# Row sets by a table of places, blocks turned one by one at the peer head, operands shifted within 256 bytes

## The chip, the cores and the metric

The kernel is one program on one core of one Trainium2 chip. TensorE (PE) multiplies, VectorE (DVE) and ScalarE (ACT) work elementwise, GpSimd (POOL) issues the gathers, SyncE (SP) the other transfers; sixteen DMA engines move the data. The metric is the device time of one execution in microseconds. Before the change: median 2463.3 us of three runs (2456.23 to 2467.06).

## What is computed

One step of a streaming encoder in fp32 over 384 tokens: 256 of a prompt and 8 x 16 of running streams (the sample), 1024 wide. Layer 0 is a Mamba-2 mixer and a PEER channel mixer, layer 1 windowed attention and a PEER channel mixer; a norm ends it. The PEER part (128 x 128 experts, 8 heads, 16 picks each) is where most of the time goes:

```python
q = (xb @ w_q).reshape(PEER_TOKEN_BLOCK, PEER_HEADS, PEER_QDIM)
s1 = jnp.einsum('thd,nd->thn', q[..., :PEER_HALF], sub_k1)
s2 = jnp.einsum('thd,nd->thn', q[..., PEER_HALF:], sub_k2)
v1, i1 = lax.top_k(s1, PEER_TOPK)
v2, i2 = lax.top_k(s2, PEER_TOPK)
cand = (v1[..., :, None] + v2[..., None, :]).reshape(PEER_TOKEN_BLOCK, PEER_HEADS, PEER_TOPK * PEER_TOPK)
vs, ci = lax.top_k(cand, PEER_TOPK)
...
ue = jnp.take(u_tab, eid, axis=0)
act = jax.nn.gelu(jnp.einsum('tkd,td->tk', ue, xb).astype(jnp.float32))
ve = jnp.take(v_tab, eid, axis=0)
return jnp.einsum('tk,tkd->td', (gate * act).astype(xb.dtype), ve)
```

## The kernel before

**Stages.** Mixer, peer layer 0, attention, peer layer 1, final norm, one after the other. The tokens are three blocks of 128 (`NB`): two of the prompt, the third the sample.

**Products.** An fp32 product is made of three in the type fp32r: each operand is split in a rounded part `hi` and a rest `lo`, and hi·hi, hi·lo and lo·hi are summed in PSUM. `split` is two instructions, a copy on ACT (L130) and a subtraction on DVE (L131). Weights come in tiles of 512 KB, which SP issues (L150) into four `raw` buffers; `hi` and `lo` have two buffers each, and a third (`hix`, `lox`) where the dictionary `more` lends one. `gemm_cols` (L166 to L168) has the weights as the stationary operand and the activations as the moving one; `gemm_rows` (L179) the other way round.

**The mixer's and the attention's end.** The last product leaves the layer's result in six PSUM banks, two for each block. Behind it DVE adds them to the stream `h`: six instructions at L651 (mixer) or L914 (attention).

**A peer layer's head.** `rstd_of` (L192) gives 1/rms of each block: squares on ACT (L200), a sum on DVE (L202, L203), a power on POOL (L204). L951 norms a block, L968 transposes it on TensorE (24 transposes, eight banks), and `split` makes `qhi` and `qlo` of each bank. `exact` (L963, ACT) keeps an unsplit copy `xf`. Then sixteen column tiles of query products (`ct` 0 to 15, 384 columns) run, with the routing's top-16 on DVE beside and behind them.

**The U stage** is 128 steps, s = 0 to 127: in each a weight tile of the prompt's u table is loaded, split and multiplied with `qhi`/`qlo` (from s near 64 on with `xhi`/`xlo`). **The V stage** is another 128 steps, s = 128 to 255: the step's gated activations (`phi`, `plo`, from the array `G`) times a tile of the v table, into four PSUM banks of the prompt. Some tiles are *native*: unsplit fp32 (L1360).

**The sample's rows.** Each of the sample's 128 tokens has 128 picked experts, so rows are gathered by index instead: POOL issues indirect transfers (`gather`, L1168) of 128 rows of 4 KB, 0.5 MB each. 128 gathers bring u rows into three buffers `gath`, and DVE multiplies each (L1212, `u_item`). For v there are two ways. Of the 32 numbers r, 24 make *sets*: four gathers into free places of `G` (`fetch_v`), then eight matmuls of TensorE (`v_quad`, L1272) behind a small mask (`quad_prep`). The remaining eight r are 32 *items*: one gather each (`fetch_item`), and a multiply-add into `acc` on DVE (`v_item`, L1237); when the last is in, a mask is made (L1242, L1243) and TensorE reduces `acc` (L1247, `items_end`).

**What sets the order.** Tables at the head of the file say at which step s each thing is due: `U_DUE` (points of a line: so many u rows by such a step), `V_DUE` (the step of each set), `I_DUE` (first and last step of the items), `AHEAD` (up to which step the third weight buffer is lent). `tick`, `quads` and `item_tick` read them at each step. A place in the second half of `G` is free until the U step that fills it with gates, one in the first half from the V step on that has used them; `v_bufs` and the first line of `fetch_v` say which place the n-th row takes. The U stage's second half and the V stage run inside `in_order`, which fixes the order as written on PE, DVE and ACT (`HELD`); POOL and SP are not held. Elsewhere the framework's scheduler places the instructions; `behind` is one of its priorities.

Buffers lie in each partition in the order in which they are allocated, and with the sizes used here `xhi`, `xlo`, `qhi` and `qlo` all begin at a multiple of 256 bytes; so do their slices, 1024 or 1536 bytes apart.

## Time and profile before

| | us |
|---|---|
| median of three runs | 2463.3 (2456.23 to 2467.06) |
| the profiled execution | 2448.66 (its span 2447.0, mean granted TensorE clock 0.988) |
| mixer | 0 to 389 |
| head and query products of peer 0 | 389 to 502 |
| U stage, peer 0 | 502 to 895 |
| V stage, peer 0 | 895 to 1336 |
| attention | 1336 to 1492 |
| head and query products of peer 1 | 1492 to 1608 |
| U stage, peer 1 | 1608 to 1997 |
| V stage, peer 1 | 1997 to 2436 |
| final norm | 2436 to 2447 |

The table's stages are cut by hand, where the first matmul of the next kind stands. In the rows of the profile, times are microseconds from the span's start; a row names the engine, the line, the operation, the buffers (out<-in), the count, and in brackets the idle time ahead of it and what ended it. PEld is the loading of the stationary operand, which overlaps PE. The chain is the work that ended last, followed back from the end.

### The profile page before, as it was taken

The numbers are of one execution on the slowest core, as the hardware profiler recorded it, in microseconds if no ns is written. First come the engines' busy times: TensorE is split into PE (matmuls) and PEld (weight loads), VectorE is DVE, ScalarE is ACT, GpSimd is POOL, SyncE is SP. The second block draws the span as 40 slices with busy tenths as digits, with TensorE's granted clock in tenths as the row PEclk, the third lists the DMA queues.
The fourth block names the chain that finished last, engine by engine and source line by source line (L and its number), as shares of the span: only waits on it lengthen the run. The fifth ranks groups of instructions, "written<-read, shape, count | busy, mean of one in ns | idle before, by whom it ended". The sixth has DMA issues, their size and how long they took to land.

```text
span 2447.0 us, 44417 instructions
## 1 busy us (share of the span) xinstructions
PE 2356.0 (96%) x16592; PEld 2022.8 (83%) x16592; DVE 1967.0 (80%) x4237; ACT 1250.5 (51%) x2428; POOL 772.4 (32%) x779
## 2 busy tenths in 40 slices
PE   8999999999999999998998998999999999998997
PEld 7899988999998896666776777999998896666775
DVE  5988845979998999888775576979998998878775
ACT  5656524434476666454443554344476666554443
POOL 2222200012145434665442100011245435655540
PEclk9999999999999999999999999999999999999999
DMA  5555434466799889999994514456799889999994
GB/s 201 173 186 179 157 131 150 132 208 235 242 331 350 316 308 342 396 403 375 359 386 140 158 63 157 137 209 240 242 330 360 309 305 345 394 409 370 367 379 147
DMA packets 177080, 649.76 MB, mean 266 GB/s; under 512 B 21136, under 2 KB 23040, under 8 KB 174208
## 3 DMA queue, kind: packets, MB, share of 16 engines
q1 hardware_dynamic: 99936, 365.85, 41.7%
q0 software_dynamic: 76928, 281.07, 30.7%
q8 instruction: 130, 2.13, 0.3%
q14 instruction: 86, 0.70, 0.1%
HBM read 630.62 MB, written 18.06 MB: 265 GB/s over the span
## 4 chain that ended last, share of the span: by engine, by line
PE 65%; DMA 8%; DVE 5%; issue 3%; POOL 2%; ACT 2%; POOLq 0%; DVEq 0%; ACTq 0%
PE bank L179 20%; PE bank L166 11%; PE bank L168 11%; PE bank L167 11%; DMA gath<-in_p_u,eidU 4%; PE bank L1272 3%; PE bank L1360 2%; PE bank L1285 2%; PE bank L1327 2%; DVE lo L131 2%; DMA G<-in_p_v,eidU 1%; DMA G<-in_p_v,eidT 1%; POOL G L1168 1%; DMA G<-xrow 1%; DMA h<-hd 1%
## 5 line engine op out<-in xcount | busy, mean ns | idle before, releaser
L130 ACT CAST hi<-raw 128x1024 fp32r<-128x1024 f32 (+1 forms) x492 | 512.1, 1042 | 703.7 <-PE bank L167 373.8
L131 DVE TENSOR_TENSOR lo<-raw,hi 128x1024 fp32r<-128x1024 f32 (+1 forms) x492 | 595.4, 1211 | 170.0 <-ACT hi L130 165.3
L1168 POOL DMA_INDIRECT gath<-in_p_u,eidU x256 | 328.6, 1284 | 796.0 <-DVE gath L1212 448.4
L168 PE MATMUL bank<-xhi,lo 128*128 128x256 f32 (+1 forms) x1344 | 399.8, 297 | 8.6 <-DVE lo L131 8.6
L166 PE MATMUL bank<-xhi,hi 128*128 128x256 f32 (+1 forms) x1344 | 407.2, 303 | 0.0
L167 PE MATMUL bank<-xlo,hi 128*128 128x256 f32 (+1 forms) x1344 | 397.8, 296 | 0.0
L166 PE MATMUL bank<-qhi,hi 128*128 128x256 f32 (+1 forms) x896 | 272.9, 305 | 7.4 <-ACT xf L963 7.4
L168 PE MATMUL bank<-qhi,lo 128*128 128x256 f32 (+1 forms) x896 | 269.2, 301 | 1.0 <-DVE lo L131 0.9
L167 PE MATMUL bank<-qlo,hi 128*128 128x256 f32 (+1 forms) x896 | 269.6, 301 | 0.0
L1168 POOL DMA_INDIRECT G<-in_p_v,eidT x192 | 223.8, 1166 | 144.4 <-PE bank L1272 86.9
L168 PEld LDWEIGHTS bank<-xhi,lo 128*128 128x128 f32 x1344 | 256.6, 191 | 13.1 <-DVE lo L131 12.8
L166 PEld LDWEIGHTS bank<-xhi,hi 128*128 128x128 f32 x1344 | 256.9, 191 | 12.6 <-issue 7.1
L167 PEld LDWEIGHTS bank<-xlo,hi 128*128 128x128 f32 x1344 | 257.1, 191 | 0.3
L1212 DVE SCALAR_TENSOR_TENSOR gath<-gath,G 128x1024 f32<-128x1024 f32 x128 | 156.0, 1220 | 77.1 <-DMA gath<-in_p_u,eidU 76.8
L1315 ACT ACTIVATE oa<-ioh,e2T 128x128 f16<-128x128 f16 x512 | 163.3, 390 | 92.2 <-PE bank L1327 90.8
L179 PE MATMUL bank<-hi,phi 128*128 128x512 f32 x640 | 205.7, 403 | 0.2
L130 ACT CAST hix<-raw 128x1024 fp32r<-128x1024 f32 x104 | 109.1, 1049 | 188.4 <-PE bank L179 103.8
L179 PE MATMUL bank<-lo,phi 128*128 128x512 f32 x640 | 199.1, 392 | 3.6 <-DVE lo L131 3.6
L179 PE MATMUL bank<-hi,plo 128*128 128x512 f32 x640 | 197.7, 390 | 0.0
L166 PEld LDWEIGHTS bank<-qhi,hi 128*128 128x128 f32 x896 | 172.5, 193 | 8.1 <-ACT xf L963 7.9
L168 PEld LDWEIGHTS bank<-qhi,lo 128*128 128x128 f32 x896 | 172.4, 192 | 1.4 <-DVE lo L131 1.4
L131 DVE TENSOR_TENSOR lox<-raw,hix 128x1024 fp32r<-128x1024 f32 x104 | 126.9, 1221 | 57.4 <-ACT hix L130 57.3
(373 smaller groups left out, 4953.9 us busy)
## 6 DMA issues: line engine op xcount, KB each, us to landing
raw<-in_u_t SPq DMA_DIRECT2D x256, 512.0 KB, 4.6
raw<-in_p_v SPq DMA_DIRECT2D x256, 512.0 KB, 6.3
raw<-in_w_in SPq DMA_DIRECT2D x32, 512.0 KB, 4.2
raw<-in_p_w_q SPq DMA_DIRECT2D x32, 512.0 KB, 3.2
raw<-in_w_z SPq DMA_DIRECT2D x16, 512.0 KB, 5.2
s<-in_state_ssm SPq DMA_DIRECT2D x8, 1024.0 KB
out_sm_ssm<-s SPq DMA_DIRECT2D x8, 1024.0 KB, 5.2
raw<-in_w_out SPq DMA_DIRECT2D x16, 512.0 KB, 3.2
```

What stands on the lines that cost most here:

```text
L130: act.copy(hi, raw)
L131: dve.tensor_tensor(lo, raw, hi32, op=OP.subtract)
L166: pe.matmul(ps, whi[:, s], xhi[:, k, c0:c1], start=(k == 0), stop=False)
L167: pe.matmul(ps, whi[:, s], xlo[:, k, c0:c1], start=False, stop=False)
L168: pe.matmul(ps, wlo[:, s], xhi[:, k, c0:c1], start=False, stop=(k == KD - 1))
L179: mm = pe.matmul(ps, x, w[:, hf * n:(hf + 1) * n], start=s_, stop=e_)
L1168: pool.indirect_dma_start(out=tile_, out_offset=None, in_=tab, in_offset=bass.IndirectOffsetOnAxis(ap=idx, axis=0))
L1212: pin(dve.scalar_tensor_tensor(tile_, tile_, 1.0, xg[g], op0=OP.mult, op1=OP.mult, accum_out=au[g][:, j:j + 1]))
L1272: pe.matmul(out_s[hf][32 * q:32 * q + 32, :], cm[:, q], rows[q][:, hf * 512:hf * 512 + 512], start=(r == 0), stop=False, tile_position=(0, ...
L1285: pe.matmul(ps, wt[0][:, k * P:(k + 1) * P], xf[:, k], start=(k == 0), stop=(k == KD - 1))
L1315: act.activation(a[:, i], ioh, AF.Square, scale=-1.0, bias=e2T[:, t, 0:1])
L1327: pe.matmul(ps[:, i], ones[i // 4][:, i % 4], eg[:, i, j], start=(j == 0), stop=(j == 1))
```

## The change

Four parts, in the order of the diff.

1. *Tables and places.* The sets are due in three stretches: six in the U stage, seven from step 149 on, eleven from step 196 on (before 5, 11 and 8, from 83, 148 and 206 on). The places are now a table of their own, `V_SLOTS`: six in the second half of `G` from U step 36 on, eight in the first half from V step 133 on, each with the steps between which it may be used; `v_slot` gives a row the first one that is free, and `taken` holds those in use. One row is fetched at a step at most (before two). The line of u rows has more points, the items start six steps later and end four later, and the third weight buffer is lent three steps longer.
2. *The peer head.* The mixer and the attention hand their last add over (`hold["add"]`). The head does it block by block, inside `in_order`: add, squares, sum, power, norm, transposes, then the next block. The first weight tile is split ahead of it, with the third `hi`/`lo` buffer already lent. The query products of the first two column tiles (`ahead`) stand between the splits of the eight `k`. For the other tiles `behind` goes.
3. *The items' mask* is made when item 30 of 32 is in, in `items_sel`.
4. *Phases.* Small unused tiles are allocated ahead of or behind the operands. The mixer's `xhi`/`xlo` now begin 64 bytes past a multiple of 256, `qhi` 192, `qlo` 160, the peer's `xhi` 192 and `xlo` 224. The others stay at 0.

```diff
+I_DUE = (192, 250)
+AHEAD = 2 * 64 - 5
+U_DUE = ((64, 22), (71, 27), (78, 33), (104, 53), (128, 72), (148, 87), (196, P))
+V_DUE = ([82, 86, 90, 94, 98, 103] + [149 + 6 * i for i in range(7)] + [196 + 9 * (i // 2) for i in range(11)])
+V_SLOTS = [(1, 36 + 4 * i, 66, 100 + 4 * i) for i in range(6)] + [(0, e, 128 + e + 5, 256) for e in (0, 4, 8, 12, 20, 24, 28, 32)]
...
+            T(xp_pool, [P, 16], F32, tag="gap0")
             xhi = T(xp_pool, [P, KD, NT], F32R, tag="xhi")
             xlo = T(xp_pool, [P, KD, NT], F32R, tag="xlo")
+            T(xp_pool, [P, 48], F32, tag="gap1")
...
-                for b in range(NB):
+                def add(b):
                     for hf in range(2):
                         hh = h[:, b, hf * 512:(hf + 1) * 512]
                         dve.scalar_tensor_tensor(hh, accs[b][hf], rs[:, b:b + 1], hh, op0=OP.mult, op1=OP.add)
+
+                hold["add"] = add
...
+            gap = lambda n, i: T(qpool, [P, n // 4], F32, tag=f"gap{i}")
             sk = T(qpool, [P, 2, P], F32, tag="sk")
             sync.dma_start(sk, t_in["sub_k"][l])
+            gap(192, 0)
             qhi = T(qpool, [P, KD, NT], F32R, tag="qhi")
+            gap(224, 1)
             qlo = T(qpool, [P, KD, NT], F32R, tag="qlo")
+            gap(96, 2)
...
-            rr = rstd_of(h)
-            xn = []
-            for b in range(NB):
-                xn.append(qTp[:, 4 * b:4 * b + 4].rearrange("p c t -> p (c t)"))
-                after["dve"] = dve.tensor_scalar(xn[b], h[:, b], rr[:, b:b + 1], None, op0=OP.mult)
...
+            more.update(hi=(lpool, 1), lo=(lpool, 1))
+            turn_of.update(hi=1, lo=1)
+            raws = [load_raw(t_in["p_w_q"][l, ct]) for ct in range(2)]
...
+            def squares(b):
+                for hf in range(2):
+                    hh = slice(hf * 512, hf * 512 + 512)
+                    act.activation(xn[b][:, hh], h[:, b, hh], AF.Square, scale=1.0 / 32, accum_out=s2[:, b, hf:hf + 1])
+
+            def normed(b, parts):
+                c = slice(b, b + 1)
+                dve.scalar_tensor_tensor(ss[:, c], s2[:, b, 0:1], EPS, s2[:, b, 1:2], op0=OP.add, op1=OP.add)
+                pool.tensor_tensor(rr[:, c], ss[:, c], mhalf[:, c], op=OP.pow)
+                for i in range(parts):
+                    w = slice(i * D // parts, (i + 1) * D // parts)
+                    dve.tensor_scalar(xn[b][:, w], h[:, b, w], rr[:, c], None, op0=OP.mult)
...
+            with in_order():
+                wq = [split_raw(raws[0])]
+                for b in range(NB):
+                    add(b)
+                    squares(b)
+                    normed(b, 1 + (b == 2))
+                    if b < 2:
+                        turn(range(2 + 2 * b), [0] if b == 0 else [1])
+                    if b == 1:
+                        turn((2, 3), [0])
...
-            for k in range(KD):
-                ps = bank([P, NT])
-                for b in range(NB):
-                    pe.transpose(ps[:, b * P:(b + 1) * P], xn[b][:, k * P:(k + 1) * P], ident)
-                turned.append(ps)
-                split(qhi[:, k], qlo[:, k], ps, scale=gcol[:, 2 + l, k:k + 1])
-                if k == 1:
-                    exact(0)
...
+            with in_order():
+                turn((4, 5), [0, 1])
+                turn(range(6), [2])
+                ahead = [bank([P, NT]) for _ in range(2)]
...
+                act.copy(hi1, raws[1])
+                for k in range(KD):
+                    ready(k)
+                    if k in (1, 2):
+                        exact(k - 1)
+                    ks = slice(k * P, (k + 1) * P)
+                    pe.matmul(ahead[0], wq[0][0][:, ks], qhi[:, k], start=(k == 0), stop=False)
+                    pe.matmul(ahead[1], hi1[:, ks], qhi[:, k], start=(k == 0), stop=False)
+                    pe.matmul(ahead[0], wq[0][0][:, ks], qlo[:, k], start=False, stop=False)
+                    pe.matmul(ahead[1], hi1[:, ks], qlo[:, k], start=False, stop=False)
+                    pe.matmul(ahead[0], wq[0][1][:, ks], qhi[:, k], start=False, stop=(k == KD - 1))
+                    if k in (1, 2):
+                        turn([k + 5], range(NB))
+                for k in range(2, KD):
+                    exact(k)
+                dve.tensor_tensor(lo1, raws[1], hi1.bitcast(F32), op=OP.subtract)
+                for k in range(KD):
+                    pe.matmul(ahead[1], lo1[:, k * P:(k + 1) * P], qhi[:, k], start=False, stop=(k == KD - 1))
...
-                half, e = (1, HE - 20 + 4 * (n % 4)) if s < 2 * HE else (0, 4 * (n % v_bufs(s)) + (4 if n % v_bufs(s) > 3 else 0))
...
+            def v_slot(n, s):
+                return next((k for *k, s0, s1 in V_SLOTS if s0 <= s and V_DUE[n // 4] <= s1 and tuple(k) not in taken), None)
...
-            def items_end():
+            def items_sel():
...
+                    if done["i"] == TG - 2:
+                        items_sel()
...
-                last = 4 * V_FIRST if s < 2 * HE else 4 * len(QR)
-                ahead = 4 * done["v"] + (4 if s < 2 * HE else v_bufs(s))
-                for _ in range(2):
-                    n = done["f"]
-                    if n < min(ahead, last) and (n < 4 * V_FIRST or s > 2 * HE + 4 + 4 * (n % 4)):
-                        fetch_v(n, s)
-                        done["f"] += 1
+                first = 4 * sum(d < 2 * HE for d in V_DUE)
+                if s % 4 == 3 and s < V_DUE[0]:
+                    return
+                if done["f"] < (first if s < 2 * HE else 4 * len(QR)) and v_slot(done["f"], s):
+                    fetch_v(done["f"], s)
+                    done["f"] += 1
...
                     xhi = T(xp, [P, KD, NP], F32R, tag="xhi")
+                    T(xp, [P, 8], F32, tag="gap")
                     xlo = T(xp, [P, KD, NP], F32R, tag="xlo")
...
-                if e2 >= 7:
+                if e2 >= 2:
                     quads(HE + e2)
```

What moves on three engines follows; lines of the changed file from 653 on lie 2 to 76 further down.

DVE at the first peer head, before: `h` is the stream, `ss` a block's mean square, `qTp` the normed block. Adds of the later blocks (L651) stand ahead of the first block's norm (L951).

```order
L651 SCALAR_TENSOR_TENSOR h_95<-bank_3484,rs_3953,h_95 128x512
L202 TENSOR_TENSOR ss_3989<-ss_630_3990 128x1
L203 TENSOR_SCALAR ss_3989<-ss_3989 128x1
L651 SCALAR_TENSOR_TENSOR h_95<-bank_3485,rs_3953,h_95 128x512
L651 SCALAR_TENSOR_TENSOR h_95<-bank_3486,rs_3953,h_95 128x512
L951 TENSOR_SCALAR qTp_3987<-h_95,rstd_3991 128x1024
```

The same place after (L653 is the add, L976 the sum, L980 the norm):

```order
L131 TENSOR_TENSOR lox_3999<-raw_3991,hix_3998 128x1024
L653 SCALAR_TENSOR_TENSOR h_95<-bank_3485,rs_3955,h_95 128x512
L653 SCALAR_TENSOR_TENSOR h_95<-bank_3486,rs_3955,h_95 128x512
L976 SCALAR_TENSOR_TENSOR ss_3995<-ss_637_3996 128x1
L980 TENSOR_SCALAR qTp_3986<-h_95,rstd_3997 128x1024
L653 SCALAR_TENSOR_TENSOR h_95<-bank_3487,rs_3955,h_95 128x512
```

A block is normed ahead of the next block's add, and the first weight split stands ahead of all of it.

POOL in the V stage of layer 0, where sets and u rows are gathered, before: `G<-in_p_v,eidT` is a row of a set, `gath<-in_p_u` a u row.

```order
L1168 DMA G_624_3979<-in_p_v,eidT_3975 128x1024 x4
L1168 DMA gath_11979<-in_p_u,eidU_3968 128x1024
L1168 DMA G_624_3979<-in_p_v,eidT_3975 128x1024
L1168 DMA gath_12015<-in_p_u,eidU_3968 128x1024
L1168 DMA gath_12063<-in_p_u,eidU_3968 128x1024
L1168 DMA G_624_3979<-in_p_v,eidT_3975 128x1024 x4
L1168 DMA gath_12099<-in_p_u,eidU_3968 128x1024
```

After, the queue there:

```order
L1233 DMA G_626_3975<-in_p_v,eidT_3971 128x1024 x4
L1233 DMA gath_11929<-in_p_u,eidU_3964 128x1024
L1233 DMA G_626_3975<-in_p_v,eidT_3971 128x1024
L1233 DMA gath_11968<-in_p_u,eidU_3964 128x1024
L1233 DMA gath_12005<-in_p_u,eidU_3964 128x1024
L1233 DMA gath_12046<-in_p_u,eidU_3964 128x1024
L1233 DMA gath_12125<-in_p_u,eidU_3964 128x1024
L1233 DMA G_626_3975<-in_p_v,eidT_3971 128x1024 x5
```

There are four u rows between two groups of set rows where there were one or two; the set rows still stand four and five in a row.

DVE at the last items of layer 1, before: L1237 is an item, `cm` the mask, L131 the splits of the weights and of the gates.

```order
L131 TENSOR_TENSOR lo_27180<-raw_27177,hi_27179 128x1024
L131 TENSOR_TENSOR plo_27184<-G_3436_20031,phi_27183 128x256
L1237 SCALAR_TENSOR_TENSOR G_2848_16531<-G_2848_16531,cU_16522 128x1024
L1242 MEMSET cm_27200 128x128
L1243 TENSOR_REDUCE cm_27200<-ident_69 128x4x8
L131 TENSOR_TENSOR lo_27226<-raw_27223,hi_27225 128x1024
```

After (L1303 the item, L1308 and L1309 the mask):

```order
L1303 SCALAR_TENSOR_TENSOR G_2847_16522<-G_2847_16522,cU_16513 128x1024
L1308 MEMSET cm_27212 128x128
L1309 TENSOR_REDUCE cm_27212<-ident_69 128x4x8
L131 TENSOR_TENSOR lox_27218<-raw_27215,hix_27217 128x1024
L131 TENSOR_TENSOR plo_27222<-G_3432_20023,phi_27221 128x256
L131 TENSOR_TENSOR lo_27240<-raw_27237,hi_27239 128x1024
L131 TENSOR_TENSOR plo_27244<-G_3432_20023,phi_27243 128x256
L1303 SCALAR_TENSOR_TENSOR G_2847_16522<-G_2847_16522,cU_16513 128x1024 x2
L131 TENSOR_TENSOR lo_27284<-raw_27281,hi_27283 128x1024
```

The mask has moved ahead of two weight splits, and the last two items stand together.

## The prediction

> **What bounds the kernel now.** The page comes first: the engines' shares, the chain that ended last, the sizes of the transfers.

> ```profile
> PE 2356.0 (96%) x16592; PEld 2022.8 (83%) x16592; DVE 1967.0 (80%) x4237; ACT 1250.5 (51%) x2428; POOL 772.4 (32%) x779
> ...
> PE 65%; DMA 8%; DVE 5%; issue 3%; POOL 2%; ACT 2%; POOLq 0%; DVEq 0%; ACTq 0%
> ...
> raw<-in_p_v SPq DMA_DIRECT2D x256, 512.0 KB, 6.3
> ```

> TensorE works or is waited for nearly always, so only two things shorten the kernel: its remaining waits, and a shorter matmul. DMA is second in the chain. So I looked next where TensorE stands still and DMA ends the wait: the V stage (the 128 V steps of a peer layer). These are its steps 24 to 71 of layer 0 (s = 152 to 199 in the code), and two later stretches, for the product matmuls alone; the columns are the stretch, its length, busy time (count) of PE and PEld, the granted clock, the DMA share, GB/s.

> ```profile
> 975.20:1162.00 186.80, 122.47 (x492) 92.28 (x493) 0.98 0.99 392
> 1209.40:1260.50 51.10, 44.10 (x194) 35.88 (x193) 1.00 0.95 369
> 1260.50:1282.20 21.70, 21.70 (x97) 17.98 (x96) 1.00 1.01 397
> ```

> The last row is eight undisturbed steps: 96 matmuls in 21.70 us, 0.226 us each. The middle one is sixteen steps (192 matmuls, 43.4 us) with four sets of v rows: (51.1 - 43.4) / 4 = 1.92 us a set. The other work of the first stretch follows, by line: native V tiles (L1360), the row sets (L1272, 16 records each), the gate products (L1327), POOL's gathers (L1168).

> ```profile
> 975.20:1162.00 186.80, 25.63 (x56) 10.23 (x56) 0.98 0.99 392
> 975.20:1162.00 186.80, 22.64 (x160) 4.74 (x160) 0.98 0.99 392
> 975.20:1162.00 186.80, 12.37 (x309) 10.34 (x305) 0.98 0.99 392
> 975.20:1162.00 186.80, 110.50 (x90) 0.98 0.99 392
> ```

> TensorE needs 492 x 0.226 + 25.6 + 12.4 + 10 x 1.92 = 168.4 us there, but the stretch lasts 186.8: 18.4 us are lost. DMA needs (90 gathers + 48 weight tiles) x 0.524 MB = 72.4 MB, at 392 GB/s 184.6 us. **The stretch runs at DMA's pace**, at a share of 0.99. How the loss looks at its worst point, on PE and then on DVE:

> ```profile
> 1139.01 0.61 PE L179 MATMUL bank<-hix,phi 128*128 128x512 f32 x2
> 1145.53 1.22 PE L179 MATMUL bank<-lox,phi 128*128 128x512 f32 x2 [5.90 <-DVE lox L131]
> 1146.55 1.05 PE L179 MATMUL bank<-hix,plo 128*128 128x512 f32 x2
> 1147.40 1.05 PE L179 MATMUL bank<-hix,phi 128*128 128x512 f32 x2
> ...
> 1143.10 1.23 DVE L1212 SCALAR_TENSOR_TENSOR gath<-gath,G 128x1024 f32<-128x1024 f32 x1 [6.27 <-DMA gath<-in_p_u,eidU]
> ```

> VectorE, whose order is fixed, stands 6.27 us at an item for its late row; the split of the next weight tile stands behind it, and TensorE behind that. After it, pairs of matmuls begin 0.85 us apart (1146.55, 1147.40) instead of 2 x 0.226 = 0.45.

> **The change part by part.** *Row sets.* Stepping through both versions' tables gives, for s = 152 to 199, 89 gathers before (the trace shows 90) and 78 now: 38 u rows, 33 v rows, 7 item rows; 8 sets instead of 10. TensorE's need falls to 168.4 - 3.8 = 164.6 us, DMA's to (78 + 48) x 0.524 = 66.1 MB, 168.5 us at 392 GB/s. DMA still ends last, by 4 us: gain 186.8 - 168.5 = 18.3. What was removed comes back at s = 200 to 239: 8 sets instead of 6, 54 gathers instead of 45. TensorE needed 480 x 0.226 + 6 x 1.92 = 120.0 and needs 123.8 us now; DMA (54 + 40) x 0.524 = 49.3 MB, 125.7 us. Cost 5.7. Net 12.6 us a layer; the same stretch of layer 1 also has 492 such matmuls in 186.8 us: **-25 us** for both. The ends come from the rate. At 397 GB/s (the 1260.50 row) the two stretches take 166.4 and 124.2: -16 a layer, -32. At 371 / 0.97 = 382 (the 120 us after the first stretch, 371 GB/s at a share of 0.97) they take 173 and 129: -4.9 a layer, -10. I take 392, the rate of the stretch itself.

> ```profile
> 1162.00:1282.20 120.20, 109.70 (x481) 89.88 (x481) 1.00 0.97 371
> ```

> [...]

> In the U stage's second half six sets stand where five stood, with six places instead of four, so two rows can be fetched a set earlier. Item and row gathers share POOL's queue there as well.

> ```profile
> PE bank L168 <- DVE lo L131: 4.1, 6, 1.3
> ```

> This wait (all of that half in layer 0: 4.1 us, 6 times) is what can go. DMA's load there grows by one gather in s = 80 to 103, so I take 1 us a layer, **-2**; ends -8 and +4 (as much lost as there is now, halved).

> *The last items.* TensorE's reduction of the items waits for a mask that VectorE makes behind the last item, once in each layer:

> ```profile
> 1304.26 1.92 PE L1247 MATMUL bank<-G,cm 128*32 128x512 f32 x16 [1.76 <-DVE cm L1243]
> 2404.55 1.92 PE L1247 MATMUL bank<-G,cm 128*32 128x512 f32 x16 [1.76 <-DVE cm L1243]
> ...
> 2402.68 1.28 DVE L1237 SCALAR_TENSOR_TENSOR G<-G,cU 128x1024 f32<-128x1024 f32 x1
> ```

> The mask is made two items earlier now. The last two items stand between two splits, 2 x 1.28 us after a split that ends about 2.8 us into a step of 2.72 us, which is 0.1 us ahead of the second step's end. The wait goes: **-3.5**; ends -3.5 and 0. Giving up the third weight buffer three steps later moves the reload of h with it; the add that waits for it stays between two splits, at no cost.

> *The head.* Between the last mixer product and the first query product (layer 0, then layer 1):

> ```profile
> 380.63 1.41 DVE L651 SCALAR_TENSOR_TENSOR h<-bank,rs,h 128x512 f32<-128x512 f32 x2 [1.12 <-PE bank L179]
> 382.83 0.16 DVE L202 TENSOR_TENSOR ss<-ss 128x1 f32<-128x1 f32 x1 [0.79 <-ACT bank L200]
> ...
> 384.63 0.74 DVE L951 TENSOR_SCALAR qTp<-h,rstd 128x1024 f32<-128x1024 f32 x1
> ...
> 389.95 2.35 DVE L131 TENSOR_TENSOR lo<-raw,hi 128x1024 fp32r<-128x1024 f32 x2
> ...
> 390.09 1.09 PE L968 MATMUL bank<-ident,qTp 128*128 128x128 f32 x8 [0.74 <-DVE qTp L951]
> ...
> 383.25 0.54 POOL L204 TENSOR_TENSOR rstd<-ss,mhalf 128x1 f32<-128x1 f32 x1 [51.46 <-DVE ss L203]
> ...
> 390.50 3.88 ACT L133 ACTIVATE qhi<-bank,gcol 128x384 fp32r<-128x384 f32 x8 [0.37 <-issue]
> ...
> 394.99 0.69 PE L166 MATMUL bank<-qhi,hi 128*128 128x384 f32 x1 [3.81 <-ACT xf L963]
> ...
> 1486.19 1.29 DVE L914 TENSOR_TENSOR h<-h,bank 128x512 f32<-128x512 f32 x2 [1.05 <-PE bank L179]
> ...
> 1491.22 0.61 PE L179 MATMUL bank<-hi,olo 128*128 128x512 f32 x2
> 1500.85 0.69 PE L166 MATMUL bank<-qhi,hi 128*128 128x384 f32 x1 [3.58 <-ACT xf L963]
> ```

> Now VectorE does a block to its end before the next one's add: 1.41 (add), 0.79 (the square's tail), 0.16 (one sum instead of two), POOL with both hops about 0.7, 0.74 (norm): 3.8 us. What is late next is VectorE itself: from 380.7 the third block's first half is normed at 380.7 + 3 x 3.8 - 0.4 = 391.7, six transposes and one split of 3.88 / 8 = 0.49 follow, and the first product can start near 392.5, 2.5 us earlier than 394.99. Two of eight columns are turned between products, six transposes of 0.11 us (the eight of the row at 390.09 lie 0.11 apart and last 1.09 together), 0.66 us. Gain 1.9; layer 1, from 1486.2 by the same sum, 2.4. Both: **-4**. The first two weight tiles' splits (2.35 us of VectorE at 389.95, between norm and splits) move ahead of the adds or behind the splits, under running products.

> ```profile
> 395.00:399.50 4.50, 4.50 (x14) 4.50 (x15) 2.63 (x4) 2.50 (x7) 0.00 (x0) 0.50 0.26 100
> 2196.00:2198.30 2.30, 0.28 (x9) 0.31 (x10) 2.27 (x6) 0.00 (x0) 1.99 (x2) 1.00 0.99 397
> 2198.40:2201.70 3.30, 3.30 (x16) 2.71 (x14) 3.30 (x6) 1.63 (x4) 0.89 (x2) 0.50 1.03 413
> ```

> The head's first products run at a granted clock of 0.50 for 4.5 us, which costs 2.3. The new idle pieces are shorter, about 2 us each, with transposes between. But the other two rows show a wait of 2 us that was followed by 0.50 as well, so I leave that cost as it is; ends: gone in both heads (-9 in all), or twice as long (+1).

> [...]

> *Phases.* The moving operands of 3 x (1024 + 640 + 256 + 256) matmuls in the peer layers and 3 x 256 in the mixer start 32 to 224 bytes past a multiple of 256 instead of on it: 7296 in all.

> ```profile
> L166 PE MATMUL bank<-xhi,hi 128*128 128x256 f32 x1024 | 295.6, 289 | 0.0
> L166 PE MATMUL bank<-qhi,hi 128*128 128x256 f32 x640 | 184.2, 288 | 0.0
> L166 PE MATMUL bank<-qhi,hi 128*128 128x384 f32 x256 | 88.8, 348 | 7.4 <-ACT xf L963 7.4
> L166 PE MATMUL bank<-qhi,hix 128*128 128x256 f32 x256 | 74.2, 290 | 0.0
> ```

> No row has such an operand off phase 0. The nearest are equal shapes whose buffers lie elsewhere: 288, 289, 290 ns. So I take 0, with ends of 2 ns each way, 15 us either way.

> **Sum.** -25 - 2 - 3.5 - 4 = -34.5 us. The profiled execution took 2448.66 us (span 2447.0), which becomes 2414. The median of the three runs is 2463.3, 14.6 above it, and I carry that distance: **2429**.

> **Rivals.** *The rate is lower where rows and items come together* (s = 200 to 239), 382 GB/s: V gives -10, time 2444. For it speaks 371 at a share of 0.97, against it 397 in the same stretch. 15%. *Slower: the same mechanism below its turning point.* Both stretches hold 115.4 MB and lasted 306.8 us, so V gains nothing at 376 GB/s, and the kernel is 12 us slower at 363. [...] Against it speak 392 and 397; no busy stretch shows less. 5%. *Phases matter:* 2 ns less, 2414, 9%; 2 ns more, 2444, 8%. Speaking for either is only that every operand lies at 0 now. *The sets move, but not the load:* POOL's order is not fixed by hand, and if its row gathers still leave in clumps of four or five ahead of item rows, items are late as now, and only head and mask remain: 2456, 7%. The forecast has 56%.

> All ends low together give 2396, all high 2476; they are independent, and about 21 us around 2429 holds most of the forecast's own case. With the rivals at 2444 and the runs' spread of 5 us: 2404 to 2453. A measurement of this kernel can tell about 0.5% (12 us) from no change. Faster by more than that: 82%; within: 13%; slower: 5%.

> **What would show it.** Right: the steps that now lie between 975 and 1162 take some 168 us with DMA still at a share near 1; no PE wait of several us for a split there; the late stretch a little longer; no wait at the item reduction; the first query product 2 us earlier after the last mixer product. The mixer's order of instructions is unchanged, so its 389 us show the phases alone. Wrong: matmul pitches other than 0.12 and 0.226 us, a DMA rate that falls in the late stretch, or waits as long as now at u rows.

## The result and the profile after

The changed kernel takes 2442.3 us (median of five runs, 2438.17 to 2446.07) against 2456.23 (five runs, 2455.66 to 2467.06): ratio 0.9921, interval [0.9902, 0.9939]. Compared again on another occasion it gave 0.9939 [0.9919, 0.9959]. The forecast was 2429, 34.5 us less than before. How large the gain is depends on the measure: 19 us by the ratio on record, 14 by the two medians (their quotient is 0.9943), 10.5 between the profiled executions (span 2447.0 and 2436.5).

The page of the changed kernel, engines and chain:

```profile
PE 2345.2 (96%) x16591; PEld 2011.4 (83%) x16592; DVE 1965.2 (81%) x4233; ACT 1249.7 (51%) x2428; POOL 747.7 (31%) x779
...
PE 80%; DVE 7%; DMA 5%; issue 4%; ACT 3%; POOL 1%; another core or an unknown queue 0%; POOLq 0%; SPq 0%; ACTq 0%; DVEq 0%
```

The chain before begins only at 388 us and its shares add up to 85% of the span, so the two pages are compared as parts of their chains: DMA went from 9% (8 of 85) to 5%, TensorE from 76% (65 of 85) to 80. Some of the DMA waits went, but the span hardly followed. The stretches of the V stages show it. The rows are V steps 24 to 71 of layer 0, 72 to the first matmul of 127, 72 to 111 of these by themselves, then 24 to 71 of layer 1; columns as in the prediction with all five engines:

```profile
967.10:1151.50 184.40, 172.62 (x996) 118.23 (x993) 147.92 (x248) 88.89 (x177) 92.66 (x82) 0.95 0.95 360
1151.50:1320.20 168.70, 168.45 (x816) 126.39 (x814) 120.68 (x153) 74.04 (x112) 67.76 (x55) 1.00 0.91 355
1151.50:1276.20 124.70, 124.53 (x610) 93.34 (x609) 89.71 (x112) 53.82 (x80) 64.88 (x52) 1.00 1.02 407
2070.00:2252.40 182.40, 168.15 (x996) 116.33 (x993) 148.00 (x248) 88.58 (x177) 94.01 (x82) 0.98 0.95 365
```

The early stretch became 2.4 and 4.4 us shorter (186.8 before) where 18.3 were forecast. Its traffic did fall as forecast: 184.4 us at 360 GB/s are 66.4 MB. But the DMA engines' rate fell with it, from 392 to 360, at a share of 0.95: **DMA's rate no longer set the pace, and something else did.** In the same stretch, VectorE, then POOL, then TensorE:

```profile
1026.62 1.22 DVE L1278 SCALAR_TENSOR_TENSOR gath<-gath,G 128x1024 f32<-128x1024 f32 x1 [6.24 <-DMA gath<-in_p_u,eidU]
...
1016.98 1.26 POOL L1233 DMA_INDIRECT gath<-in_p_u,eidU  x1 [0.30 <-issue]
1018.55 1.17 POOL L1233 DMA_INDIRECT gath<-in_p_u,eidU  x1 [0.30 <-issue]
1020.02 1.17 POOL L1233 DMA_INDIRECT gath<-in_p_u,eidU  x1 [0.31 <-issue]
1028.12 0.94 POOL L1233 DMA_INDIRECT gath<-in_p_u,eidU  x1 [6.93 <-DVE gath L1278]
...
1031.33 1.01 PE L1403 MATMUL bank<-og,oa 128*128 128x64 f16 x16 [4.33 <-DVE og L1379]
```

VectorE stands 6.24 us at an item for its u row, as it did before the change. The three buffers' rows had been asked for at 1016.98 to 1020.02, and the first was there at 1026.6, nearly 10 us later; the next request (1028.12) had to wait until an item freed a buffer. So at most three rows are on their way.

A wait cost more than its length here. Stretches of 3.4 us of that place, in order: length, PE, PEld, DVE, ACT, POOL, granted clock, DMA share, GB/s:

```profile
979.10:982.50 3.40, 1.24 (x25) 0.85 (x28) 3.37 (x8) 0.73 (x3) 0.94 (x1) 1.00 1.03 413
982.50:985.90 3.40, 3.40 (x15) 0.75 (x7) 3.40 (x7) 2.42 (x5) 1.24 (x2) 0.50 0.94 365
996.20:999.60 3.40, 1.97 (x18) 1.38 (x17) 3.37 (x7) 0.00 (x0) 0.00 (x0) 1.00 1.02 418
999.60:1003.00 3.40, 3.40 (x25) 2.71 (x22) 3.10 (x7) 2.34 (x7) 1.40 (x2) 1.00 1.04 387
```

A stretch with TensorE 36% busy is followed by one at 0.50, one with 58% by one at 1.00. The early stretch of layer 0 had a mean clock of 0.95, which is at most 9 us of TensorE's work; before it was 0.98, at most 4.

The matmuls did become shorter. Three undisturbed U steps (72 fp32r matmuls of 256 columns), before and after:

```profile
604.52:613.16 8.64, 8.64 (x74) 1.00 0.52 174
```

```profile
596.12:604.60 8.48, 8.48 (x75) 1.00 0.51 176
```

That is 0.1200 and 0.1178 us each.

At the items' reduction TensorE no longer waits (no idle time is given in its row), and at the heads one step came earlier and one later. PE rows of the heads of both layers, and the ACT row that began the second:

```profile
385.14 0.38 PE L989 MATMUL bank<-ident,qTp 128*128 128x128 f32 x2
391.65 0.44 PE L1028 MATMUL bank<-qhi,hix 128*128 128x384 f32 x1 [0.15 <-ACT qhi L133]
...
1305.58 1.92 PE L1317 MATMUL bank<-G,cm 128*32 128x512 f32 x16
...
1479.35 0.61 PE L179 MATMUL bank<-hi,olo 128*128 128x512 f32 x2
1483.11 0.41 PE L989 MATMUL bank<-ident,qTp 128*128 128x128 f32 x2 [3.15 <-DVE qTp L980]
1486.67 2.37 PE L989 MATMUL bank<-ident,qTp 128*128 128x128 f32 x10 [3.16 <-DVE qTp L980]
1491.07 0.67 PE L1028 MATMUL bank<-qhi,hix 128*128 128x384 f32 x1
...
1480.00 0.63 ACT L972 ACTIVATE qTp<-h 128x512 f32<-128x512 f32 x1 [7.04 <-PE bank L179]
```

Layer 0: 6.6 us from the last mixer product to the first query product instead of 9.0. Layer 1: 11.3 (1479.8 to 1491.1) instead of 9.2. There the first square waits for the last attention product: squares now write into `qTp`, and their wait ends with the products whose operands they seem to overwrite, while before they wrote into a PSUM bank. The three blocks then follow each other 3.2 to 3.6 us apart.

### The profile page after: what moved, and what is told of

It reads as the page before. It is cut to its first block, busy times and chain, and to the rows that moved or that the text cites. A ratio compares the mean times of both kernels' runs of the same rounds, so it can differ in the third digit from the quotient of the medians.

```text
span 2436.5 us, 44422 instructions
## 1 busy us (share of the span) xinstructions
PE 2345.2 (96%) x16591; PEld 2011.4 (83%) x16592; DVE 1965.2 (81%) x4233; ACT 1249.7 (51%) x2428; POOL 747.7 (31%) x779
## 4 chain that ended last, share of the span: by engine, by line
PE 80%; DVE 7%; DMA 5%; issue 4%; ACT 3%; POOL 1%; another core or an unknown queue 0%; POOLq 0%; SPq 0%; ACTq 0%; DVEq 0%
PE bank L179 24%; PE bank L166 13%; PE bank L168 13%; PE bank L167 12%; DMA gath<-in_p_u,eidU 5%; PE bank L1348 3%; PE bank L1361 2%; PE bank L1403 2%; DVE lo L131 2%; PE bank L1436 2%; DVE gath L1278 1%; ACT hi L130 1%; PE bank L533 1%; PE bank L472 1%; PE bank L473 1%
## 5 line engine op out<-in xcount | busy, mean ns | idle before, releaser
L130 ACT CAST hi<-raw 128x1024 fp32r<-128x1024 f32 (+1 forms) x476 | 495.4, 1041 | 728.8 <-PE bank L167 324.2
L131 DVE TENSOR_TENSOR lo<-raw,hi 128x1024 fp32r<-128x1024 f32 (+1 forms) x476 | 575.7, 1210 | 193.8 <-ACT hi L130 166.2
L166 PE MATMUL bank<-xhi,hi 128*128 128x256 f32 (+1 forms) x1344 | 407.1, 303 | 0.9 <-issue 0.9
L168 PE MATMUL bank<-xhi,lo 128*128 128x256 f32 (+1 forms) x1344 | 398.0, 296 | 9.4 <-DVE lo L131 8.2
L168 PEld LDWEIGHTS bank<-xhi,lo 128*128 128x128 f32 x1344 | 255.2, 190 | 14.9 <-DVE lo L131 12.9
L166 PEld LDWEIGHTS bank<-xhi,hi 128*128 128x128 f32 x1344 | 253.9, 189 | 16.1 <-issue 8.7
L1233 POOL DMA_INDIRECT G<-in_p_v,eidT x192 | 213.7, 1113 | 141.1 <-PE bank L1348 76.1
L166 PE MATMUL bank<-qhi,hi 128*128 128x256 f32 (+1 forms) x784 | 232.9, 297 | 0.0
L168 PE MATMUL bank<-qhi,lo 128*128 128x256 f32 (+1 forms) x784 | 228.6, 292 | 2.0 <-DVE lo L131 2.0
L167 PE MATMUL bank<-qlo,hi 128*128 128x256 f32 (+1 forms) x784 | 229.6, 293 | 0.0
L179 PE MATMUL bank<-lo,phi 128*128 128x512 f32 x632 | 198.5, 395 | 9.2 <-DVE lo L131 9.0
L179 PE MATMUL bank<-hi,phi 128*128 128x512 f32 x632 | 205.5, 406 | 0.2
L130 ACT CAST hix<-raw 128x1024 fp32r<-128x1024 f32 x118 | 123.7, 1048 | 152.1 <-PE bank L167 70.2
L179 PE MATMUL bank<-hi,plo 128*128 128x512 f32 x632 | 196.2, 392 | 0.0
L1278 DVE SCALAR_TENSOR_TENSOR gath<-gath,G 128x1024 f32<-128x1024 f32 x128 | 155.9, 1218 | 36.6 <-DMA gath<-in_p_u,eidU 33.2
L1278 DVE SCALAR_TENSOR_TENSOR gath<-gath,xg 128x1024 f32<-128x1024 f32 x128 | 155.5, 1216 | 9.2 <-DMA gath<-in_p_u,eidU 9.2
L131 DVE TENSOR_TENSOR lox<-raw,hix 128x1024 fp32r<-128x1024 f32 x118 | 143.7, 1218 | 22.2 <-ACT hix L130 19.2
L179 PEld LDWEIGHTS bank<-hi,phi 128*128 128x128 f32 x632 | 115.0, 189 | 44.2 <-issue 18.7
## 6 DMA issues: line engine op xcount, KB each, us to landing
raw<-in_u_t SPq DMA_DIRECT2D x256, 512.0 KB
raw<-in_p_v SPq DMA_DIRECT2D x256, 512.0 KB
raw<-in_w_in SPq DMA_DIRECT2D x32, 512.0 KB
raw<-in_p_w_q SPq DMA_DIRECT2D x32, 512.0 KB
raw<-in_w_z SPq DMA_DIRECT2D x16, 512.0 KB
raw<-in_w_out SPq DMA_DIRECT2D x16, 512.0 KB
```

The costliest lines, as they stand in the source:

```text
L130: act.copy(hi, raw)
L131: dve.tensor_tensor(lo, raw, hi32, op=OP.subtract)
L166: pe.matmul(ps, whi[:, s], xhi[:, k, c0:c1], start=(k == 0), stop=False)
L167: pe.matmul(ps, whi[:, s], xlo[:, k, c0:c1], start=False, stop=False)
L168: pe.matmul(ps, wlo[:, s], xhi[:, k, c0:c1], start=False, stop=(k == KD - 1))
L179: mm = pe.matmul(ps, x, w[:, hf * n:(hf + 1) * n], start=s_, stop=e_)
```

## The experiments

All comparisons are ratios to the kernel before, run on the same chip beside each kernel. The stage table below is made from one profiled execution of each: a stage begins at the first matmul of the step named and ends at the first matmul behind it (the row "72 to 127" of the V stage ends at the first matmul of step 127).

| us | before | after | tables only | head only | four rows | POOL in order | before, four rows | all at 192 |
|---|---|---|---|---|---|---|---|---|
| V steps 24 to 71, layer 0 | 186.9 | 184.3 | 186.8 | 187.9 | 164.4 | 180.1 | 188.9 | 165.6 |
| V steps 24 to 71, layer 1 | 186.8 | 182.3 | 181.4 | 184.8 | 164.3 | 177.7 | 191.9 | 165.9 |
| V steps 72 to 111, layers 0, 1 | 120.2, 120.2 | 124.7, 124.6 | 124.0, 124.0 | 120.2, 120.2 | 124.0, 124.0 | 130.0, 129.9 | 120.2, 120.2 | 124.0, 124.0 |
| V steps 72 to 127, layers 0, 1 | 169.3, 169.0 | 168.7, 168.6 | 172.0, 172.6 | 169.2, 169.5 | 167.9, 168.2 | 173.9, 174.0 | 169.0, 169.5 | 168.2, 168.0 |
| U steps 64 to 71, layers 0, 1 | 25.9, 25.9 | 28.4, 28.2 | 31.6, 30.5 | 26.1, 26.2 | 31.5, 32.2 | 25.8, 25.8 | 26.2, 26.2 | 28.8, 27.4 |
| U steps 72 to 127, layers 0, 1 | 194.5, 194.0 | 194.0, 197.9 | 198.4, 194.4 | 198.1, 197.3 | 190.6, 190.9 | 194.3, 193.6 | 199.0, 196.3 | 191.6, 195.8 |
| span | 2447.0 | 2436.5 | 2459.5 | 2452.4 | 2397.3 | 2431.9 | 2455.1 | 2394.7 |
| ratio of the runs | 1 | 0.9921 | 1.0015 | 0.9995 | 0.9803 | 0.9915 | 1.0010 | 0.9725 |

One execution can differ from the next of the same kernel by several us in these stages. The early V stretches took 186.2 and 186.5 us in a second profiled execution of the changed kernel, 179.9 and 181.9 without the gaps, 186.8 and 190.6 with the gaps alone in the kernel before.

**The addresses alone, and all but the addresses.** Taken out of the changed kernel, and put into the one before; every engine's order stays.

```diff
-            T(xp_pool, [P, 16], F32, tag="gap0")
...
-            gap(192, 0)
             qhi = T(qpool, [P, KD, NT], F32R, tag="qhi")
-            gap(224, 1)
...
-                    T(xp, [P, 8], F32, tag="gap")
                     xlo = T(xp, [P, KD, NP], F32R, tag="xlo")
+                    fill(xp)
```

> The changed kernel with all operands back at phase 0; every engine's order of instructions is the changed kernel's. Theory A (the addresses carry the gain: by the traces 2688 query and early U matmuls of 256 columns became 2.0 ns shorter, 3072 late U ones 1.1 ns, 576 of the mixer 4.8 ns, 11 us in all): the time goes back to that of before, 2453 us, span 2447, pitches 120 ns again. Theory B (tables and head carry it, as forecast): it stays at 2442, within 4 us, whatever the pitches.

> The kernel before with the gap tiles alone; every engine's order is that of before. Theory A: pitches of 113 to 121 ns as in the changed kernel, 11 us less than before, about 2445. Theory B: within 4 us of before, 2456. A third possibility (A'): the matmuls are shorter but the stretches that wait for rows take it back, 4 to 7 us less.

Without the gaps: 0.9971 [0.9951, 0.9992]. The gaps alone: 0.9973 [0.9955, 0.9991], 7 us. Theory B's strict form falls (the addresses do shorten the kernel), and so does A's (the rest is not worth nothing): each is a third to a half of the gain.

**The tables alone, the head alone,** each put into the kernel before:

```diff
-V_DUE = [83 + 5 * i for i in range(5)] + [148 + 4 * i for i in range(11)] + [206 + 12 * (i // 2) for i in range(8)]
+V_DUE = ([82, 86, 90, 94, 98, 103] + [149 + 6 * i for i in range(7)] + [196 + 9 * (i // 2) for i in range(11)])
...
```

> The kernel before with the new tables, places and fetch rules alone (mask, head and phases as before). Theory A: no gain; by the changed kernel's stages the U stage's second half loses 4 us (layer 0) and 8 us (layer 1) and the V stage gives 4 to 5 a layer back: 2452 to 2460. Theory B: the forecast's 25 to 27 us less, 2430; its lower end for the V stages, 10 less, would be 2446.

> The kernel before with the new head alone. Forecast: 4 us less. By the changed kernel's stages (from the last mixer product to the first query product 2.4 us less in layer 0, 2.1 more in layer 1 with 3.4 us of half clock, the query products 1 us longer each time): nothing in sum, within 3 us of before. If the half clock of before at 505 to 516 us also goes here, 3 to 4 us less.

Tables: 1.0015 [1.0000, 1.0030]. Head: 0.9995 [0.9980, 1.0010]. **Neither shortens the kernel by itself.** With the tables alone the early stretch stayed at 186.8 us in layer 0 and fell to 181.4 in layer 1, and the late ones grew by some 3 us. The three parts multiply to about 0.998, the whole is 0.992 to 0.994. The mask was not tried alone, so whether it or the parts' interplay makes the difference stays open.

**The changed kernel again:**

> The changed kernel itself, beside the next ones and compared again. If the first comparison holds: 0.990 to 0.994 of before. If it was a lucky draw of where the half-clock windows fall: 0.994 to 0.998, which is what the parts alone (0.997, 0.997, 1.0015, 0.9995) would rather add up to.

0.9939: at the border of the two. The profiled execution spanned 2441.9 us, with the same instructions, and had a lower clock. The spans and mean clocks, after and again:

```profile
core 0: 2436.5 us, clock 0.985
```

```profile
core 0: 2441.9 us, clock 0.981
```

1.5% and 1.9% of the span are 37 and 46 us of clock, given away in twice as much time at a granted clock of 0.50. That does not account for each stretch: in the early V stretch of layer 0 the mean clock was no lower than the first time (0.96 and 0.95), and it still took 186.2 us instead of 184.3.

**A fourth buffer for u rows,** lent in the V stage:

```diff
+            vp, nf = [], [2]
...
-                    urows[k] = gather(T(one, [P, D], F32, tag="gath", bufs=3), t_in["p_u"], eidU[:, g, j:j + 1])
+                    tile_ = T(vp[0], [P, D], F32, tag="gx", bufs=1) if vp and k % 4 == 3 else T(one, [P, D], F32, tag="gath", bufs=3)
+                    urows[k] = gather(tile_, t_in["p_u"], eidU[:, g, j:j + 1])
...
-                    fetch_u(done["u"] + 2)
+                    while nf[0] <= done["u"] + 2 + len(vp):
+                        fetch_u(nf[0])
+                        nf[0] += 1
...
+            vp.append(lpool)
             stage = [(wt, ph)]
```

> The changed kernel with a fourth buffer for u rows in the V stage (lent beside the third weight buffer), so that a row is asked for one item earlier; the traffic is the same. Theory D (the forecast's: the early V stretch, steps 24 to 71, runs at the DMA engines' pace): it keeps its 184 and 182 us within 2 us, and the time stays. Theory L (a row is asked for only when the third one before it is used, queues behind set rows and weight tiles, and VectorE stands at it with the next weight split behind): the stretches fall to 165 to 175 us, 15 to 30 us less in all.

**Ratio 0.9803 [0.9786, 0.9819].** The two early stretches, of layers 0 and 1:

```profile
968.80:1133.20 164.40, 164.12 (x995) 114.90 (x992) 148.21 (x249) 88.76 (x177) 94.73 (x81) 1.00 1.01 402
2049.40:2213.70 164.30, 164.07 (x994) 114.86 (x991) 148.56 (x249) 88.69 (x177) 93.86 (x81) 1.00 1.01 401
```

TensorE is busy throughout at full clock, and DMA moves the same 66 MB at 402 GB/s. Theory L holds: one row more on its way gives 18 to 20 us in each layer, far more than two executions differ.

**GpSimd in order:**

```diff
-HELD = (mybir.EngineType.PE, mybir.EngineType.DVE, mybir.EngineType.Activation)
+HELD = (mybir.EngineType.PE, mybir.EngineType.DVE, mybir.EngineType.Activation, mybir.EngineType.Pool)
```

> The changed kernel with GpSimd's order fixed as written too, so that one set row goes out at a step between u rows, instead of four or five at once; the traffic is the same. Theory D: the stretches keep 184 and 182 us. Theory C (the clumps make u rows late): 5 to 15 us less in each. Against both: GpSimd stands at a place of G that is not free yet, u rows queue behind it, and the stretches are longer than now.

0.9915 [0.9900, 0.9929]. The early stretches were 4.2 and 4.6 us shorter than in the first execution of the changed kernel, just below theory C's range, and 6.1 and 8.8 shorter than in its second, inside it. The late ones were 5 us longer, with waits of TensorE for set rows at their begin (3.0 us in each layer). Clumps are part of the V stage's lateness, not its core. At U steps 64 to 71 they are all of it: 25.8 us here, as before the change, against 27.4 to 33.2 in every other execution with the new tables.

**Four rows in the kernel before:**

> The kernel before with the fourth u-row buffer of the V stage alone (old tables, old head, phases 0). Theory L: its early V stretches lost their 18 us to late rows too and fall from 186.8 to TensorE's need, 168 to 172 us, 30 to 37 us less in all, 2415 to 2422; the new tables are then worth 2 sets, 4 us, a layer there and nothing else. Theory D2 (with the old tables' 72.4 MB the DMA engines bind at the 392 to 402 GB/s seen so far): the stretches stay at 180 to 185 us, 4 to 14 us less in all, and the tables' lighter load is what lets the fourth buffer work.

1.0010 [0.9992, 1.0028]: nothing. The early stretches:

```profile
975.40:1164.20 188.80, 177.29 (x1025) 117.83 (x1022) 149.82 (x249) 88.53 (x177) 105.19 (x89) 0.98 0.98 387
2077.90:2269.80 191.90, 178.40 (x1025) 118.46 (x1022) 149.78 (x249) 88.58 (x177) 107.17 (x89) 0.96 0.97 380
```

With the old tables' 73 MB the DMA engines are at 380 to 387 GB/s and a share of 0.97 to 0.98, and asking earlier does not help. Theory L falls there; theory D2 has the direction, but its 180 to 185 us and its gain of 4 to 14 us did not come either. At the 402 GB/s of the run above, 73 MB would take 182 us. The other 7 to 10 us are not explained by bytes; TensorE waits there once behind a weight split (6.8 and 6.1 us) and several times for set rows (3.1 and 6.5 us in all). **What is shown is that the two have to go together:** the old tables' gathers and the three buffers each keep the stretch long. Either edit alone moved nothing (1.0015 and 1.0010); with both it is 22 us a layer shorter than before. That bytes are the whole of the first limit is not shown.

**A sweep of phases by itself,** then the best phase in the kernel.

> Not the model: 118 groups of 48 fp32r matmuls (triples as in the kernel) on operands at chosen phases within 256 bytes, nothing else running, no output but a corner of one. Theory P (the pitch follows from the phases of the two operands alone): the kernel's own pitches come back within 1 ns: 256 columns 120 ns with all at 0, 113 to 115 with the stationary operand at 64 and the moving one at 0, 118 with moving 192/160, 119 with 192/224; 384 columns 173 at 0, 175 with moving at 192; 512 columns 227 at 0. Theory Q (something else in the kernel made them shorter): 120, 173 and 227 at every phase.

The sweep has 115 groups. Windows of single ones (from the first start to the 48th): 256 columns all at 0; moving operands at 192/160, 192/192; 512 columns all at 0, moving at 192, both at 192:

```profile
46.08:51.80 5.72, 5.72 (x51) 1.00 0.00 0
358.89:364.52 5.63, 5.63 (x50) 1.00 0.00 0
364.78:370.20 5.42, 5.42 (x50) 1.00 0.02 3
...
791.51:802.28 10.77, 10.77 (x51) 1.00 0.01 2
723.52:734.57 11.05, 11.05 (x50) 1.00 0.00 0
824.93:835.69 10.76, 10.76 (x51) 1.00 0.01 2
```

Divided by 47: 0.1217, 0.1198, 0.1153; 0.2291, 0.2351, 0.2289 us. So in the sweep the phase of the moving operand *against that of the stationary one* mattered: at 512 columns the moving one alone at 192 gave 0.2351, both at 192 gave 0.2289, near the 0.2291 of both at 0. With the moving operands shifted to 192, or to 192 and 160, 256 columns gain 2 to 6 ns; at 192, 512 columns lose 6 and 384 (8.26 and 8.23 us a group) hardly move. Theory Q falls; P holds in kind but not to 1 ns (stationary at 64: 0.1194, and 0.113 to 0.115 in the mixer), so more than the two phases decided. Each phase had one buffer in the sweep, so there it is not separated from the rest of its address.

```diff
             gap(192, 0)
             qhi = T(qpool, [P, KD, NT], F32R, tag="qhi")
-            gap(224, 1)
             qlo = T(qpool, [P, KD, NT], F32R, tag="qlo")
-            gap(96, 2)
+            gap(320, 1)
...
                     xhi = T(xp, [P, KD, NP], F32R, tag="xhi")
-                    T(xp, [P, 8], F32, tag="gap")
                     xlo = T(xp, [P, KD, NP], F32R, tag="xlo")
+                    T(xp, [P, 8], F32, tag="gap")
```

> The changed kernel with four u rows, and with qhi, qlo and the peer's xhi, xlo all at phase 192. By the sweep (113 to 115.5 ns for 256 columns where both moving operands are at 192 and the stationary one at 0, 119 to 121 elsewhere): 2 to 4 ns less for 5760 matmuls, 12 to 23 us less than with four rows alone, 2377 to 2389. By the changed kernel's own rows where a 192 follows a 192 (115.6 for x, 118.5 for q): 8 us less, 2393. If the gain hangs on other bits of the addresses: nothing, 2401.

0.9725 [0.9702, 0.9749], **the fastest version tried**, 68 us under before. The same three U steps as above:

```profile
596.36:604.52 8.16, 8.16 (x74) 1.00 0.47 163
```

8.16 / 72 = 0.1133, where the sweep's group mean was 0.1153 and its single pitches mostly 0.113. Against four rows alone (0.9803, on another chip) that is 19 us by the ratios, inside the expected 12 to 23, but the two intervals leave room for 9 to 29. The profiled executions differ by only 2.6 us (spans 2397.3 and 2394.7), since the U stage's second half did not get shorter there (last column of the table): in layer 1 TensorE waits 5.6 us for weight splits, up to 2.7 at a time, where the execution with four rows alone had 0.7.

**TensorE kept busy in the heads:**

```diff
                 for b in range(NB):
+                    if b < 2:
+                        for _ in range((14, 24)[l]):
+                            pe.matmul(turned[0][:, 2 * P:], ident, ident, start=True, stop=True)
                     add(b)
```

> The changed kernel with four u rows, and with idle TensorE pieces of the peer heads filled by transposes of the identity that nothing reads (2 x 14 in layer 0, 2 x 24 in layer 1). Theory W (the clock is granted for 3.41 us at a time, half where TensorE worked less than about 0.45 of the stretch before): the half clock in heads and query products goes, 1.7 to 3.4 us in layer 0 and 3.4 to 5.1 in layer 1, so 4 to 8 us less than with four rows alone, 2393 to 2397. Against it: the clock falls all the same, or the added work delays the real transposes, 2400 to 2402.

> The changed kernel with four u rows, all of qhi, qlo and the peer's xhi, xlo at phase 192, and the heads' idle pieces filled with half as many products as before (2 x 7 and 2 x 12, since one of them showed as two records, 0.23 us together). If the parts add: 0.9725 of before with rows and phases, and 2 to 6 us less through heads and query products without half clock (82 and 85 us instead of 82 and 86), 0.970 to 0.972. If the filling only moves the half clock to the next weak stretch or delays the transposes: 0.972 to 0.974.

With 14 and 24: 0.9774 [0.9748, 0.9801], not to be told from four rows alone (0.9803 [0.9786, 0.9819]). Theory W's 3.41 us is the step of the half-clock records in these traces (3.413 us); its 0.45 is an estimate: of the stretches shown for the changed kernel the one 0.36 busy was followed by 0.50, the one 0.58 busy by 1.00, and the last section counts the rest. Its first half agrees with this execution: the clock stayed at 1.00 through both heads and query products, and its mean was 0.993 against 0.987 with four rows alone. But one such product lasts 0.23 us (two records of 0.117), not the 0.11 that the edit counted on, so each fill was twice as long as meant and both heads grew by 1.7 to 1.8 us. With half as many, phases and rows: 0.9749 [0.9726, 0.9773], not to be told from 0.9725 without them. Neither head grew, one stretch of half clock was left in the second layer's query products, and the time did not shorten measurably.

## Why the prediction was right or wrong

The time lay in the range and on the forecast side, with a gain of 10 to 19 us by the measure taken, some third to a half of the 34.5. That it lay there is in good part luck: the term that carried the forecast, 25 us in the V stage, gave nothing in the stretches it was worked out for, and what came was in part booked at nothing (7 us by the phases). The 14.6 us carried from the profiled execution to the median came from three runs; five runs have their median 7.6 above it.

*V stage, forecast -25.* This is the step that failed: "DMA still ends last, by 4 us: gain 18.3". Traffic fell to 66.4 MB (66.1 forecast), and TensorE's need was right: 164.6 forecast, 164.4 and 164.3 in the run with four rows, where the rate was even better than 392. But in the changed kernel the stretch took 184.3 and 182.3, because the waits at u rows had a second cause beside DMA's pace. The prediction's own sign of being wrong, "waits as long as now at u rows", came: 6.24 us against 6.27. The prediction quoted both waits of this kind (VectorE 6.27 us, TensorE 5.90 us behind it) and read them as the *form* of the bandwidth loss. A share of 0.99 did not show that fewer bytes would take less time: with fewer, the rate fell from 392 to 360. How far ahead a row is asked for (three buffers, each freed by an item in VectorE's fixed order) was in the code and was left out. The fourth rival, "the load doesn't move", named the sign (clumps ahead of item rows) with 7%; the run in order shows the clumps as a part only.

*The late stretch, forecast +5.7,* came as +4.5 and +4.4: V steps 72 to 111 took 124.7 and 124.6 us against 120.2. The step was nearly right, but not by its reason. DMA did not end last there: it moved 407 GB/s, above the 392 assumed, and TensorE was busy 124.53 of 124.70 us, so its own 123.8 set the time. By the same row the rival of a lower rate where rows and items come together (382) falls. So the two stretches together took 309.0 and 306.9 us against 307.1 and 307.0, and the V term was worth nothing where it was summed. Behind step 111 some 5 us a layer came back, which no part of the sum has as a whole: the sum was cut at s = 239, and behind it there is one set less (1.92 us), no wait at the reduction (1.76) and no wait of 1.2 to 1.4 us for a weight split.

*U stage, forecast -2.* From U step 64 to the V stage it grew from 220.4 to 222.4 and from 219.9 to 226.1 us, though its matmuls became shorter. Executions of one kernel differ by some 4 us there; the clear part is steps 64 to 71, 25.9 us before and 28.4 and 28.2 after. The sixth set costs TensorE 1.92 us later in the stage, which the term left out. And set rows now have six places free at once: between U steps 64 and 71 six of them go out together, and a u row behind them is late. VectorE and POOL in the run with four rows (which has three buffers in this stage still):

```profile
692.93 1.23 DVE L1281 SCALAR_TENSOR_TENSOR gath<-gath,xg 128x1024 f32<-128x1024 f32 x1 [4.88 <-DMA gath<-in_p_u,eidU]
...
672.73 1.99 POOL L1233 DMA_INDIRECT G<-in_p_v,eidT  x1 [0.30 <-issue]
...
680.73 1.33 POOL L1233 DMA_INDIRECT G<-in_p_v,eidT  x1 [0.30 <-DMA G<-in_p_v,eidT]
682.36 1.09 POOL L1233 DMA_INDIRECT gath<-in_p_u,eidU  x1 [0.30 <-DVE og L1382]
```

The sets' rows go out from 672.73 to 680.73; the u row is asked for at 682.36 and used at 692.93. With POOL in order a u row goes out between the set rows, and the steps take 25.8 us again, so here the clump is the cause. A fourth buffer in this stage, or POOL in order there together with four rows in the V stage, was not tried.

*The last items, -3.5.* The waits of 1.76 us are gone, as forecast. With the tables alone, mask behind the last item, the wait was 0.36 us in layer 0, so only part of the gain belongs to the mask.

*The head, -4.* Layer 0 by its own sum (2.5 forecast, 2.4 measured). Layer 1 went the other way, +2.1 instead of -2.4: the sum "by the same" missed that the squares' new target makes the first block wait for the last product. The half clock of the heads, left as it was in the sum, changed too: from 1484 on it lasted 10.24 us in layer 1, which cost 5.1, against 3.4 before (6.83 us long), and in layer 0 1.7 against 3.4 (3.41 and 6.83 us). Query products took 1 us more each (74.2 to 75.4 and 75.2). The head alone: 0.9995.

*Phases, 0 with 15 us either way.* Mis-sized, inside its bounds: -7 us by the gaps alone (interval -11 to -2), some 11 by the pitches. Mean pitches were 2 ns lower with `qhi`/`qlo` and 1.1 lower with `xhi`/`xlo` moving. The count missed the mixer's 576 matmuls with `xhi`/`xlo` stationary, which fell by 4.6 ns: there a stationary operand 64 bytes off phase was worth more than the moving ones were. The 7 us lie about midway between the forecast's 0 and the rival "2 ns less" (9%).

*DMA's rate.* The run with four rows moved 402 GB/s over 164 us, the changed kernel 407 over 125 us. Both lie above the 392 and 397 of the forecast. The rival of a slower kernel (5%) needs DMA to set the pace below 376 GB/s, and no run shows that: at the 360 of the early stretch rows were late, and one row more on its way brought 402; at the 355 of V steps 72 to 127 TensorE was busy 168.45 of 168.70 us.

*The range.* The ends called "all high 2476" add up to 2473; the range was not worked out from that figure.

## What to carry to other kernels

A stretch with DMA at a share near 1 (0.99 here) can still be late rather than full: compare bytes over time with a stretch that moves more (here 392 against 407 GB/s at 1.02, where TensorE was busy 124.53 of 124.70 us), and count how many requests the buffers let be under way, before a lighter load is booked as time. Where two limits have nearly one size, an edit of either can show nothing (1.0015 and 1.0010 here); they have to be tried together. Before operands are padded, sweep their phase against the stationary operand's for each width, since what helped 256 columns here (0.1217 to 0.1153 us in the sweep) hurt 512 there (0.2291 to 0.2351).

## What the hardware showed unasked

**A phase of 192 bytes** made 256-column fp32r matmuls 5.6% shorter (0.1200 to 0.1133 us in the kernel). Why, and what besides the two phases decides, stays open.
